# Hybrid decoder layer: the output projection and its norms join the FFN's listed order, token tiles are reordered, the third f pair's first products come earlier

## The chip, the cores and the metric

One core of one Trainium2 chip. The metric is the device time of one execution in microseconds (us), and the kernel is compared with the one before it on the same chip. TensorE (PE in the profile) multiplies, VectorE (DVE) and ScalarE (ACT) do the elementwise work, GpSimd (POOL) computes the small powers of the norms and issues accumulating DMAs, SyncE (SP) issues the other DMAs.

## The reference, cut to what matters

One layer on 1024 tokens of width 1024. The change sits between the mixing branch and the feed-forward part:

```python
merged = jax.nn.sigmoid(g_att) * y_att + jax.nn.sigmoid(g_conv) * y_conv
x = x + rms_norm(merged @ w_out[l], norm_mix_post[l])

h = rms_norm(x, norm_ffn_pre[l])
u = causal_dwconv(h @ w_up[l], conv_ffn_w[l])          # 1024 -> 2 x 2816
a, g = jnp.split(u, 2, axis=-1)
f = (jax.nn.gelu(g, approximate=True) * a) @ w_down[l]
x = x + rms_norm(f, norm_ffn_post[l])
```

## The kernel before

All products run in float16 with each operand split into a high and a low half; a product is three passes (`PASSES`): high by high, high by low, low by high. A split is one ScalarE instruction for the high half and one VectorE instruction for the low half (`split`, L98 and L99; `halves` in the FFN, L1383 and L1385). Large products are cut in two by two blocks and done with seven block products instead of eight, so sums and differences of blocks are made first.

The order of work comes about in two ways. Most of the kernel hands its instructions to the compiler's scheduler, which arranges each engine's instructions by their dependencies and by program order. Inside `tc.manual_schedule` the order of the named engines is as written. In the FFN a planner (`Plan`) writes it: every step is a job with an engine, a cost, the buffers that it reads and writes (`Buf`, each from a pool with so many tiles) and a due time; the products of TensorE have a fixed sequence (`seq=True`), and `order` places all other jobs around them by a simulation of the five engines, of the DMA and of the pools. `DUE` and `AHEAD` say how late or how early a job may be placed. TensorE's other jobs (transposes, the one-column sums `pr` over partitions) stand where that simulation finds them ready.

The passage that the change concerns, in the kernel before, is left to the compiler's scheduler:

- `wsplit("wo", ...)` splits the eight row tiles of w_out (`wh_wo`), and the last gate pair g7 finishes; `m16[k]` holds the two halves of the merged activations.
- `out_proj(tt)` for each token tile of 128: 48 matmuls into two PSUM banks `py` (L1180), ScalarE's square with a row sum (L1182), VectorE's eviction into `hn` (L1183), the first norm (a power on GpSimd, L183), the residual into `x` (L1187) and its store, the square for the second norm (L59), and the normed tile `hn` (L1190).
- `blocks(tt, h)`: eight transposes of `hn` into two banks `pt` (L1198). For tiles 0 to 3 the two halves of the blocks b11 and b21 are made (L1206, L1207); for tiles 4 to 7 the sums t1, t2, t3, t4 and b22 (L1212 to L1224), with slots `tb` and `hb`. Products 1 and 2 of a pair read tiles 0 to 3; products 3 to 7 need tiles 4 to 7 too (product 5 reads t1).
- An f pair is 128 columns of a and 128 of g of w_up. `pair_fetch`, `pair_sums` and `pair_split` load and split its weights: two staging tiles of the pool `ws` (4 tiles, shared with the x tiles `xr`), a slot `s12`, and four tiles of the pool `wh` (8 tiles). Of the first two pairs the products 1, 2 and 5 are issued here (L2089), after that the list takes over with products 6, 7, 3 and 4 (L1458). Products 1 and 2 use one bank (a), 6, 7 and 4 another (b), 5 and 3 a third (c); each product is evicted before the next one on its bank begins.

The pools that bind the passage: 16 slots `s` (eight hold w_out, four of the m16 tiles lie there), 4 tiles `x`, 4 `ws`, 8 `wh`, 8 PSUM banks.

## Time and profile before

| what | value |
|---|---|
| time, median of 3 runs | 1318.19 us (1316.74 to 1320.07) |
| the profiled execution's own time | 1317.39 us |
| its span | 1315.7 us |
| granted TensorE clock | 0.999 |
| TensorE busy | 1295.0 us |
| VectorE busy | 1096.7 us |
| ScalarE busy | 941.6 us |
| output projection's matmuls (L1180) | 602.4 to 690.3 us from the start |

Busy times are those of instructions; a matmul's end is modelled, so busy shares of TensorE are a little high, and its gaps a little larger than shown. The row of an instruction in the timeline reads: start, duration, engine, line, operation, output <- inputs, shapes, count, and in brackets the engine's idle time before it with what ended it.

### The profile page before, as it was taken

How to read it: one execution, taken by the hardware profiler on the slowest of the kernel's cores; microseconds unless marked ns; L12 is line 12 of the kernel's file. 1: busy time of each engine (PE TensorE's matmuls, PEld its weight loads, DVE VectorE, ACT ScalarE, POOL GpSimd, SP SyncE). 2: the span in 40 equal slices, each digit the busy share in tenths (PEclk: the TensorE clock that was granted, in tenths of full speed). 3: DMA queues.
4: the chain of work that ended last, by engine and by line, in shares of the span. 5: the costliest groups of instructions: out<-in, count | busy, mean ns of one | idle time of the engine just before them, and what ended most of it. 6: DMA issues, size and time to landing. Idle time of an engine off the chain costs nothing.

```text
span 1315.7 us, 16998 instructions
## 1 busy us (share of the span) xinstructions
PE 1295.0 (98%) x6406; PEld 581.5 (44%) x6406; DVE 1096.7 (83%) x1762; ACT 941.6 (72%) x1336; POOL 85.6 (7%) x120
## 2 busy tenths in 40 slices
PE   8999999999999999999999999999999999999997
PEld 4444444444444444444444444444444444444443
DVE  6578988888878967877799999789879879979986
ACT  7578878787778966675566767876977777787444
POOL 2000000000000000000110000100200210120103
PEclk9999999999999999999999999999999999999999
DMA  7111210111101223241330311611961692294807
GB/s 274 34 34 33 65 33 17 48 33 33 49 1 48 65 65 105 75 177 58 126 133 33 128 65 67 257 62 33 180 188 48 110 243 64 48 228 130 235 0 129
DMA packets 35541, 123.41 MB, mean 94 GB/s; under 512 B 4081, under 2 KB 4209, under 8 KB 35458
## 3 DMA queue, kind: packets, MB, share of 16 engines
q1 hardware_dynamic: 25088, 85.61, 19.3%
q0 software_dynamic: 10368, 36.70, 13.6%
q8 instruction: 50, 0.82, 0.3%
q14 instruction: 33, 0.27, 0.1%
q10 hardware_dynamic: 2, 0.00, 0.0%
HBM read 84.52 MB, written 37.78 MB: 93 GB/s over the span
## 4 chain that ended last, share of the span: by engine, by line
PE 54%; issue 24%; DVE 9%; DMA 6%; ACT 5%; POOL 3%; POOLq 0%; DVEq 0%; SPq 0%; ACTq 0%
PE py L1180 5%; PE pcb L212 3%; PE pcc L212 3%; PE pcx L212 3%; PE pq L212 3%; PE pk L212 3%; PE pywa L806 3%; PE pywc L806 3%; PE pd L1689 2%; PE pd L1722 2%; PE A L834 2%; POOL acc L1349 2%; PE o L834 2%; PE z L834 2%; DMA yacc<-acc 2%
## 5 line engine op out<-in xcount | busy, mean ns | idle before, releaser
L1458 PEld LDWEIGHTS <-wh_u 128*128 128x128 f16 x1776 | 172.0, 98 | 211.2 <-issue 3.3
L2089 PEld LDWEIGHTS <-wh_g 128*128 128x128 f16 x588 | 56.9, 98 | 69.4 <-issue 1.1
L1623 ACT ACTIVATE st<-pq,sd 128x512 f32<-128x512 f32 x112 | 72.3, 695 | 18.1 <-PE pq L1619 16.0
L1180 PE MATMUL py<-wh_wo,m 128*128 128x512 f16 x384 | 83.7, 379 | 0.0
L877 ACT ACTIVATE sh<-sp 128x1024 f16<-128x1024 f32 (+3 forms) x48 | 40.4, 842 | 52.2 <-DVE sp L872 52.0
L1385 DVE SCALAR_TENSOR_TENSOR wh_u<-ws_u,sc_u,wh_u 128x1024 f16<-128x1024 f32 (+1 forms) x60 | 65.5, 1102 | 7.8 <-ACT wh_u L1383 7.6
L1349 POOL DMA_DIRECT2D acc<-st x56 | 43.2, 772 | 431.1 <-ACT st L1623 430.8
L1383 ACT ACTIVATE wh_u<-ws_u,sc_u 128x1024 f16<-128x1024 f32 (+1 forms) x60 | 59.4, 1004 | 4.1 <-DVE sc_u L1368 3.9
L872 DVE TENSOR_TENSOR sp<-A,sp 1x1024 f32<-1x1024 f32 (+3 forms) x40 | 35.9, 897 | 29.9 <-PE A L834 26.5
L59 ACT ACTIVATE jk_u<-ws_u 128x1024 bf16<-128x1024 f32 x44 | 46.2, 1049 | 15.6 <-DMA ws_u<-w_up_nt 15.4
L881 DVE TENSOR_TENSOR sh<-sp,sh 128x1024 f16<-128x1024 f32 (+3 forms) x48 | 45.8, 955 | 13.5 <-ACT sh L877 13.3
L1180 PEld LDWEIGHTS <-m 128*128 128x128 f16 x384 | 37.4, 98 | 44.2
L1492 DVE SCALAR_TENSOR_TENSOR ua<-ca,cw_a,ua 128x1023 f32<-128x1023 f32 (+1 forms) x40 | 51.2, 1279 | 1.6 <-ACT ua L1490 1.5
L907 DVE SCALAR_TENSOR_TENSOR w<-e,w 128x1024 f16<-128x1024 f32 (+3 forms) x48 | 45.8, 954 | 6.8 <-ACT w L903 6.7
L1492 DVE SCALAR_TENSOR_TENSOR ug<-cg,cw_g,ug 128x1023 f32<-128x1023 f32 (+1 forms) x40 | 51.1, 1277 | 0.1
L903 ACT ACTIVATE w<-e 128x1024 f16<-128x1024 f32 (+3 forms) x48 | 40.5, 844 | 14.7 <-DVE e L898 13.7
L898 DVE TENSOR_TENSOR e<-e,g 128x1024 f32<-128x1024 f32 (+3 forms) x48 | 45.7, 953 | 2.5 <-ACT g L894 2.5
L867 ACT ACTIVATE sp<-e,one 128x1024 f32<-128x1024 f32 (+3 forms) x48 | 44.4, 925 | 4.0 <-DVE e L862 2.7
L853 ACT ACTIVATE e<-z,cz 128x1024 f32<-128x1024 f32 (+3 forms) x48 | 43.1, 898 | 3.6 <-PE z L834 3.6
L212 PE MATMUL pcb<-hT,wh_cb 128*128 128x512 f16 x192 | 45.1, 380 | 0.0
L212 PE MATMUL pcx<-hT,wh_cx 128*128 128x512 f16 x192 | 44.9, 379 | 0.0
L212 PE MATMUL pk<-hT,wh_k 128*128 128x512 f16 x192 | 44.6, 380 | 0.0
(760 smaller groups left out, 3047.6 us busy)
## 6 DMA issues: line engine op xcount, KB each, us to landing
acc<-st POOLq DMA_DIRECT2D x56, 512.0 KB, 6.2
ws_u<-w_up_nt SPq DMA_DIRECT2D x44, 512.0 KB
ds<-w_down SPq DMA_DIRECT2D x22, 512.0 KB
ws_g<-w_in_nt SPq DMA_DIRECT2D x14, 512.0 KB
x<-x SPq DMA_DIRECT2D x8, 512.0 KB
ws_wo<-w_out SPq DMA_DIRECT2D x8, 512.0 KB
xr<-x SPq DMA_DIRECT2D x8, 512.0 KB
yacc<-acc SPq DMA_DIRECT2D x16, 256.0 KB
```

The source lines that it names most:

```text
L59: self.nc.scalar.activation(self.junk(f"jk_{name}"), src, AF.Square, accum_out=acc)
L212: nc.tensor.matmul(ps, w[:, wi, ds(k * P, P)], hT[:, hi, k, ds(c * NH, NH)], start=n == 0, stop=n == last)
L806: nc.tensor.matmul(ps, w[0][:, wi, ds((d % 2) * NH + k * P, P)], acts[bi][k][:, hi, ds(c * NH, NH)], start=n == 0, stop=n == 11)
L834: nc.tensor.matmul(out, w, mv, skip_group_check=True, **kw)
L1180: nc.tensor.matmul(ps, m16[k][:, hi, ds(tt * P, P)], wo[k][:, wi, sl], start=k == 0 and p == 0, stop=k == 7 and p == 2)
L1349: j = pl.add(eng, 0.45 if eng == "SP" else 1.14, lambda: e.dma_start(dst(), srcf(), **kw), r, [b] if w is None else w, ahead=AHEAD["load"] ...
L1383: A(C["As" if big else "Ash"], lambda: act.activation(dst.t[:, 0, dsl], src.t[:, ssl], AF.Copy, scale=sb.t["s"]), [(src, sreg), sb], [(dst ...
L1385: V(C["V" if big else "Vh"], lambda: vec.scalar_tensor_tensor(dst.t[:, 1, dsl], src.t[:, ssl], sb.t["s"], dst.t[:, 0, dsl], ALU.mult, ALU. ...
L1458: pe.matmul(b.t, p.w[wt].t[:, wi, ds(wc * NH + k * P, P)], pr.block(i, h, k), start=first and n == 0, stop=n == 3 * KH - 1, skip_group_che ...
L1492: V(C["V"], lambda lag=lag: vec.scalar_tensor_tensor(u.t[:, lag:], c.t[:, :T - lag], sm.t[:, 2 - lag:3 - lag], u.t[:, lag:], ALU.mult, ALU ...
L1623: A(C["Ah"], lambda tt=tt, b=b, st=st: act.activation(st.t[:, tt % 2, :], b.t, AF.Copy, scale=q.sd.t[:, 0:1]), [b, q.sd], [(st, str(tt % 2 ...
L2089: nc.tensor.matmul(ps, w[wt][:, wi, ds(wc * NH + k * P, P)], self.block(i, hi, k), start=first and n == 0, stop=n == 3 * KH - 1, skip_grou ...
```

## The change

The output projection, its norms, the transposes and the token blocks become jobs of the planner and stand in the listed order together with the FFN; the old functions that left them to the compiler's scheduler go. The token tiles are taken in the order 0, 1, 2, 4, 3, 5, 6, 7; the first three run together, k by k. The weights of the first three f pairs are split in the list (`EARLY` lets their loads and splits be placed any time ahead). Products 1 and 2 of the third pair come ahead of the first pair's product 5, and the second pair's product 5 goes back to its place behind product 6. Three pools of small tiles get their sizes in the planner, and the planner starts with times at which the w_out tiles, the last m16 tile, ScalarE and VectorE become available. For tiles 4 to 7 the first differences read an SBUF copy of the transposed tile where they read PSUM before.

```diff
+PRE = ((0, 1), (1, 1), (0, 2), (1, 2), (2, 1), (2, 2), (0, 5))
+TORDER = (0, 1, 2, 4, 3, 5, 6, 7)
...
-        def out_proj(tt):
-            xt = xr.pop(tt)
-            sm = self.small(f"r_post{tt}")
...
-            for nh in range(2):
-                ps = self.bank(f"py{tt}_{nh}")
-                sl = ds(nh * NH, NH)
-                for k in range(8):
-                    for p, (hi, wi) in enumerate(PASSES):
-                        nc.tensor.matmul(ps, m16[k][:, hi, ds(tt * P, P)], wo[k][:, wi, sl],
-                                         start=k == 0 and p == 0, stop=k == 7 and p == 2)
-                nc.scalar.activation(jk[:, sl], ps, AF.Square, scale=sgn[:, 24:25], accum_out=sm[:, 3 + nh:4 + nh])
-                nc.vector.scalar_tensor_tensor(h[:, sl], ps, sgn[:, 24:25], gp[:, sl], ALU.mult, ALU.mult)
...
-            nc.sync.dma_start(self.x2[tt], y)
-            r2 = self.rstd_of(y, f"ffn{tt}")
-            nc.vector.scalar_tensor_tensor(h, y, r2, gf, ALU.mult, ALU.mult)
-            return h
...
-        def blocks(tt, h):
...
-            nc.vector.scalar_tensor_tensor(tb[0][:, 0], p3[0], s_h2, b11[:, 0], ALU.mult, ALU.subtract)
-            nc.vector.tensor_tensor(tb[0][:, 0], tb[0][:, 0], b11[:, 1], ALU.subtract)
-            halves(t1, tb[0][:, 0])
...
-        for tt in range(8):
-            if tt + 1 < 8:
-                load_xr(tt + 1)
-            hs[tt] = out_proj(tt)
-            if tt == 0:
-                self.pair_split("u0")
-                self.pair_fetch("u1")
-            if tt == 3:
-                self.pair_sums("u1")
-                self.pair_split("u1")
-            if tt == 5:
-                self.pair_fetch("u2")
-            for t in {2: (0,), 4: (1, 2), 5: (3, 4), 6: (5,), 7: (6,)}.get(tt, ()):
-                blocks(t, hs[t])
+        self.passage = m16, wo, xr, gp, gf, s_h2, sgn[:, 24:25]
         self.pairs = {f: Up(self, f) for f in range(NFF)}
-        p0, p1 = self.pairs[0], self.pairs[1]
-        p0.prod(1)
-        p0.prod(2)
-        p1.prod(1)
-        with tc.high_priority():
-            blocks(7, hs[7])
-        p1.prod(2)
-        p1.prod(5)
-        p0.prod(5)
 
...
+    FIRST, EARLY = 3, 200.0
...
-        pl = Plan(dict(s=16, ws=4, wh=8, o16=4, x=4, pm=8))
-        C = dict(A=0.97, Ah=0.5, As=1.04, Ash=0.6, Aq=1.18, V=1.21, Vh=0.64, Vp=0.72)
+        pl = Plan(dict(s=16, ws=4, wh=8, o16=4, x=4, pm=8, sm=8, rb=8, sc=16))
+        C = dict(Asq=0.82, A=0.97, Ah=0.5, As=1.04, Ash=0.6, Aq=1.18, V=1.21, Vh=0.64, Vp=0.72)
...
+
+        DUE = {"conv": 20.0, "fin": 25.0, "ev": 3.0, "pass": 5.0, "hn": 14.0}
...
+        m16 = [given("o16" if d < 4 else "s", t) for d, t in enumerate(m16t)]
+        wo = [given("s", t) for t in wot]
+        gp, gf = given("x", gpt), given("x", gft)
+        xr = {tt: given("ws", t) for tt, t in xrt.items()}
+        hn, prods = {}, {}
+        for k in range(8):
+            wo[k].avail = (0.0, 1.2, 4.2, 5.4, 8.0, 9.2, 10.4, 11.6)[k]
+        m16[7].avail = 13.0
+        pl.begin = {"A": 11.5, "V": 13.0}
...
+        def out_proj(tt):
...
+            for nh in range(2):
+                sl, reg, b = (lo, hi)[nh], "lh"[nh], ps[nh]
+
+                def mm(ks, b=b, sl=sl):
+                    for k in ks:
+                        for p, (h_, w_) in enumerate(PASSES):
+                            pe.matmul(b.t, m16[k].t[:, h_, ds(tt * P, P)], wo[k].t[:, w_, sl],
+                                      start=k == 0 and p == 0, stop=k == 7 and p == 2)
+                prods[tt, nh] = lambda ks, mm=mm, b=b: pl.add("PE", 0.65 * len(ks), lambda: mm(ks), [m16[k] for k in ks] +
+                                                              [wo[k] for k in ks], [b], seq=True)
+            yield
+            for nh in range(2):
+                sl, reg, b = (lo, hi)[nh], "lh"[nh], ps[nh]
+                A(C["Asq"], lambda b=b, sl=sl, nh=nh: act.activation(self.junk(f"jk_n_post{tt}")[:, sl], b.t, AF.Square,
+                                                                     scale=s_py, accum_out=sm.t[:, 3 + nh:4 + nh]),
+                  [b], [(sm, reg)], due=DUE["pass"])
+                V(C["Vp"], lambda b=b, sl=sl: vec.scalar_tensor_tensor(h.t[:, sl], b.t, s_py, gp.t[:, sl], ALU.mult, ALU.mult),
+                  [b, gp], [(h, reg)], due=DUE["pass"])
+
...
+            V(C["V"], lambda: vec.scalar_tensor_tensor(y.t, h.t, sm.t[:, 2:3], xr[tt].t, ALU.mult, ALU.add), [sm, h, xr[tt]], [y])
+            load("SP", None, lambda: self.x2[tt], lambda: y.t, r=[y], w=[], ahead=1e9)
...
+            pl.add("G", 0.6, power, [], [sm])
+            V(C["V"], lambda: vec.scalar_tensor_tensor(h.t, y.t, sm.t[:, 2:3], gf.t, ALU.mult, ALU.mult), [sm, y, gf], [h],
+              due=DUE["hn"])
...
+            def turn(e):
+                def f():
+                    for k in range(KH):
+                        pe.transpose(pt[e].t[:, ds(k * P, P)], h.t[:, ds((e * KH + k) * P, P)], self.ident)
+                return f
+            for e in range(2):
+                pl.add("PE", 0.45, turn(e), [h], [pt[e]])
...
+            for e in range(2):
+                A(C["Ah"], lambda e=e: act.activation(hbt.t[:, e], p3(e), AF.Copy, scale=s_h2), [pt[e]], [(hbt, str(e))])
+            t0, t1_ = part(tb[0], 0), part(tb[0], 1)
+            tt_(tb[0], 0, part(hbt, 0), lambda: ap["b11"][:, 0], ALU.subtract, [(hbt, "0"), (o_, "b11")])
+            tt_(tb[0], 0, t0, lambda: ap["b11"][:, 1], ALU.subtract, [(o_, "b11")])
+            two("t1", tb[0], 0)
...
         def up_weights(f):
+            ah, al, aq = (self.EARLY,) * 3 if f < 3 else (AHEAD["up"], None, AHEAD["sq"])
...
+            sq = Buf("sm", lambda: self.small(f"sm_{n}"))
+            summed = n in self.praw
+            if summed:
+                sm, ta, tg, ts = self.praw.pop(n)
+                sq = given("sm", sm)
...
-            s12 = slab(f"s12_{n}")
+            s12 = given("s", ts) if summed else slab(f"s12_{n}")
             w = p.w = [Buf("wh", lambda i=i: self.wh.tile([P, 2, D], F16, tag="wh", name=f"wh_{n}_{i}")) for i in range(4)]
...
+            if not summed:
+                comb(s12, lo, ug, lo, ug, hi, ALU.add, ahead=ah)
+                comb(s12, hi, s12, lo, ua, lo, ALU.subtract, ahead=ah)
+                comb(ug, lo, ua, lo, ug, lo, ALU.subtract, ahead=ah)
...
-            p, pr = up[f], prs[f]
-            if f < 2:
-                p.ca, p.cg, p.ug = given("s", pr.ca), given("s", pr.cg), given("s", pr.ug)
-                p.bank = {"c": given("pm", pr.ps["c"])}
-            else:
-                p.ca, p.cg, p.ug = slab(f"ca{f}"), slab(f"cg{f}"), slab(f"ug{f}")
-                p.bank = {b: Buf("pm", lambda b=b: self.bank(f"pu{f}{b}")) for b in "ac"}
-            p.bank["b"] = Buf("pm", lambda: self.bank(f"pu{f}b"))
+            p = up[f]
+            p.ca, p.cg, p.ug = slab(f"ca{f}"), slab(f"cg{f}"), slab(f"ug{f}")
+            p.bank = {b: Buf("pm", lambda b=b: self.bank(f"pu{f}{b}")) for b in "abc"}
...
-            pl.add("PE", 2.6, mm, [p.w[wt]], [b], seq=True)
+            pl.add("PE", 2.6, mm, [p.w[wt]] + [(hb[tt], BLOCK[i]) for tt in (range(4) if i < 3 else range(4, 8))], [b], seq=True)
...
-            for f in range(NFF):
-                up_weights(f) if f < 3 else None
-            for f in range(2):
+            for n, tt in enumerate(TORDER):
+                load_xr(tt)
+                if n == 0 or n >= self.FIRST:
+                    op = out_proj(tt)
+                    next(op)
+                if n >= self.FIRST:
+                    for nh in range(2):
+                        prods[tt, nh](range(8))
+                elif n == 0:
+                    rest = [out_proj(t) for t in TORDER[1:self.FIRST]]
+                    for r in rest:
+                        next(r)
+                    for k in range(8):
+                        for t in TORDER[:self.FIRST]:
+                            for nh in range(2):
+                                prods[t, nh]((k,))
+                for _ in rest.pop(0) if 0 < n < self.FIRST else op:
+                    pass
+                blocks(tt)
+                for f in {0: (0,), 2: (1,), 5: (2,)}.get(n, ()):
+                    up_weights(f)
+            for f in sorted({f for f, _ in PRE}):
                 up_open(f)
+            for f, i in PRE:
+                up_prod(f, i)
...
-                    if f >= 2:
+                    if (f, 1) not in PRE:
...
-                        if f >= 2 or i not in (5, 2):
+                        if (f, i) not in PRE:
...
-            j.t0 = 0.0
+            j.t0 = max([0.0] + [b.avail for b in j.bufs])
...
-        eng = {e: 0.0 for e in self.LAG}
+        eng = {e: self.begin.get(e, 0.0) for e in self.LAG}
```

More of the change, by code (lines that the diff above doesn't have):

```diff
@@ L1251, in mixer @@
[L1251 to L1260 removed]
+        xr = {tt: self.ws.tile([P, D], F32, tag="ws", name=f"xr{tt}") for tt in TORDER[:2]}
+        for tt in xr:
+            nc.sync.dma_start(xr[tt], a["x"][ds(tt * P, P), :])
+        self.passage = m16, wo, xr, gp, gf, s_h2, sgn[:, 24:25]
@@ L1354, in tot @@
         def tot(n, sm, cnt, slack, keep):
-            b, rb, ps, st = note(), note(), Buf("pm", lambda: self.bank(f"pr_{n}")), {}
+            b, rb, ps, st = Buf(None if keep else "sc", lambda: {}), Buf("rb", lambda: {}), Buf("pm", lambda: self.bank(f"pr_{n}")), {}
             def pre():
@@ L1397, in ffn @@
         fall = slice(0, T)
-        uw, up = {}, {}
+        up = {}
+        hb = [note() for _ in range(8)]
+        BLOCK = {1: "b11", 2: "b21", 3: "b22", 4: "t4", 5: "t1", 6: "t2", 7: "t3"}
+        m16t, wot, xrt, gpt, gft, s_h2, s_py = self.passage
+        m16 = [given("o16" if d < 4 else "s", t) for d, t in enumerate(m16t)]
[3 more added lines that the diff above has]
+        hn, prods = {}, {}
@@ L1710, in down_last @@
                 o = slab(f"o{tt}")
-                sm = Buf(None, lambda tt=tt: self.small(f"fin{tt}"))
+                sm = Buf("sm", lambda tt=tt: self.small(f"fin{tt}"))
                 y = yb_[tt]
@@ L1830, in __init__ @@
     def __init__(self, pool, make):
[L1831 removed]
+        self.pool, self.make, self.tile, self.log, self.left, self.avail = pool, make, None, [], 0, 0.0
     @property
@@ L1851, in __init__ @@
     def __init__(self, caps):
-        self.jobs, self.caps, self.now = [], caps, 0.0
+        self.jobs, self.caps, self.now, self.begin = [], caps, 0.0, {}
     def add(self, eng, cost, fn, r=(), w=(), seq=False, ahead=1e9, due=1e9):
```

124 lines of the change are left out of this document (62 added, 62 removed).

## The prediction

> **What bounds the kernel now.** I read the page first: how much of the span TensorE, the busiest engine, is without work.
>
> ```profile
> span 1315.7 us, 16998 instructions
> PE 1295.0 (98%) x6406; PEld 581.5 (44%) x6406; DVE 1096.7 (83%) x1762; ACT 941.6 (72%) x1336; POOL 85.6 (7%) x120
> ```
>
> TensorE is idle for 1315.7 - 1295.0 = 20.7 us. The change neither adds nor takes away a matmul, so it can win only a part of these 20.7 us, and lose whatever new waits it makes. The next view, busy time by stretch, says where they lie (columns: PE, PEld, DVE, ACT, POOL busy; clock; DMA).
>
> ```profile
> 0.00:20.00 20.00, 15.96 (x56) 8.07 (x57) 12.57 (x32) 15.64 (x24) 5.26 (x19) 1.00 0.88 350
> 20.00:560.00 540.00, 538.30 (x2859) 233.74 (x2858) 431.15 (x720) 408.19 (x567) 4.62 (x5) 1.00 0.16 49
> 560.00:602.00 42.00, 41.40 (x195) 18.68 (x194) 31.05 (x59) 27.07 (x42) 1.30 (x2) 1.00 0.43 154
> 602.00:634.00 32.00, 32.00 (x153) 14.78 (x152) 25.19 (x31) 20.38 (x29) 1.11 (x2) 1.00 0.21 66
> 634.00:690.00 56.00, 56.00 (x284) 28.12 (x283) 48.92 (x84) 33.75 (x65) 9.29 (x12) 1.00 0.39 132
> 690.00:712.00 22.00, 20.25 (x101) 9.78 (x100) 21.25 (x37) 14.79 (x26) 2.01 (x2) 1.00 0.14 48
> 712.00:730.00 18.00, 16.44 (x79) 7.44 (x78) 16.39 (x31) 8.78 (x10) 0.00 (x0) 1.00 0.10 30
> 730.00:1260.00 530.00, 526.30 (x2460) 238.27 (x2459) 469.56 (x699) 387.92 (x535) 48.94 (x63) 1.00 0.49 128
> 1260.00:1316.00 56.00, 48.32 (x234) 22.60 (x232) 40.59 (x75) 25.09 (x46) 13.05 (x15) 0.97 0.46 76
> ```
>
> The output projection (602 to 690) has no TensorE idle time at all: nothing can be won there, only lost. Idle are 1.75 us in 690 to 712 and 1.56 us in 712 to 730, together 3.31 us, and 3.70 us in the 530 us that the list orders already (0.7 us per 100 us). The first 602 us (4.04 + 1.70 + 0.60) lie before the change, and the 7.68 us of the last stretch are the closing chain of the last token tile, which it leaves alone. So 3.31 + 3.70 = 7.0 us are within reach, 0.5% of the time. The waits around the change, in the view of who waited for whom from 595 to 730:
>
> ```profile
> PE pt L1198 <- DVE hn L1190: 1.0, 1, 1.0
> PE pu0b L1458 <- DVE sc_u L1366: 0.8, 1, 0.8
> PE pu1b L1458 <- DVE cau L1464: 0.8, 1, 0.8
> PE pu0a L2089 <- ACT cgu L2104: 0.7, 1, 0.7
> ```
>
> **Head of the projection.** The timeline of TensorE and VectorE where it begins:
>
> ```profile
> 602.37 2.48 DVE L99 SCALAR_TENSOR_TENSOR wh_wo<-ws_wo,sc,wh_wo 128x1024 f16<-128x1024 f32 x2 [0.91 <-ACT wh_wo L98]
> 602.39 0.59 PE L1180 MATMUL py<-wh_wo,m 128*128 128x512 f16 x2
> ...
> 602.84 3.40 PE L1180 MATMUL py<-wh_wo,m 128*128 128x512 f16 x15
> ```
>
> The low half of the first w_out tile is ready only at about 602.37 + 1.28 = 603.65 (two in 2.48 us). TensorE doesn't notice: its order was chosen freely, and it runs what needs only the high half first. The new list writes the order down: for each k, for each of three tiles and two halves, the passes high-high, high-low, low-high. The second matmul needs the low half; it stood at about 602.6 and can start at 603.65. Loss: 1.05 us, once (bounds 0, if the halves come earlier, and 1.3, one whole low split). Later k don't wait: six banks times three passes are 18 x 0.216 = 3.9 us of matmuls per k (0.216 from the row below), against 1.28 us of VectorE per low half. Nor does the interleaving of three tiles win anything: the row of 15 shows matmuls running on while VectorE still makes w_out, so the old order already mixes tiles.
>
> The Trainium skill, page "TensorE: Matmul & The Clock Gate", section "Step-by-step: what each phase is for", says that matmuls stay in program order and that only weight loads are pulled ahead. By that rule the 1.05 us stand; were it wrong, the sum below would be 1.05 us lower.
>
> **Matmuls and transposes.** The counts stay:
>
> ```profile
> L1180 PE MATMUL py<-wh_wo,m 128*128 128x512 f16 x384 | 83.7, 379 | 0.0
> ...
> L1198 PE MATMUL pt<-ident,hn 128*128 128x128 f32 x64 | 8.1, 274 | 1.0 <-DVE hn L1190 1.0
> ```
>
> 384 in a row come to 83.7 us, 0.216 to 0.218 each, and 64 transposes to 8.1 us, about 1 us a tile: no difference. What changes is where the transposes stand. The list puts them where it believes the normed tile hn ready, between projection jobs of 24 matmuls (5.2 us); if hn is later than believed, TensorE stops. Tile 0's chain in the trace:
>
> ```profile
> 624.41 0.69 ACT L1182 ACTIVATE jk_n_post<-py,sgn 128x512 bf16<-128x512 f32 x1 [4.44 <-PE py L1180]
> ...
> 625.22 1.42 DVE L1183 SCALAR_TENSOR_TENSOR hn<-py,sgn,g_post 128x512 f32<-128x512 f32 x2 [2.96 <-ACT jk_n_post L1182]
> ...
> 631.02 1.28 DVE L1190 SCALAR_TENSOR_TENSOR hn<-x,r_ffn,g_ffn 128x1024 f32<-128x1024 f32 x1 [0.66 <-POOL r_ffn L183]
> ```
>
> From 624.41 to 632.30 it takes 7.9 us on free engines. The list's costs and lags for the same steps (two squares, statistics, power, residual, square, statistics, power, gain) add up to 8.8 us, so it errs on the safe side by 0.9 us, and rounding up to the next 5.2 us boundary adds on average half of that. One thing it does not know: the second row shows VectorE starting on the bank only after ScalarE's 0.69 us on it, though both only read. The Trainium skill, "PSUM — Partial Sum Buffer", section "Terms", counts two reads of one bank at once as a collision, which is the wait this row shows. That is 0.7 us inside the 0.9 us of margin. I price the risk at the rate of the stretch that is listed already, 0.7 us per 100 us over about 110 us: 0.8 us (bounds 0, and 8 us if each tile's transposes wait the 1.0 us of the first row of waits).
>
> **Norms, blocks, weights.** The same instructions as before, except that tiles 4 to 7 take the first difference from an SBUF copy: nothing on TensorE. VectorE was busy 48.92 of 56 us and 21.25 of 22 us, so I check it at the spot where TensorE first needs the last tile's t1. The timeline there: TensorE's products, the VectorE row that ends that t1 (704.59), and rows that the next part needs:
>
> ```profile
> 691.52 2.75 PE L2089 MATMUL pu0a<-hA,wh_u 128*128 128x512 f16 x12
> 694.11 2.75 PE L2089 MATMUL pu1a<-hA,wh_u 128*128 128x512 f16 x12
> 697.60 2.75 PE L2089 MATMUL pu0a<-hA,wh_u 128*128 128x512 f16 x12 [0.74 <-ACT cgu L2104]
> 701.37 1.06 PE L1198 MATMUL pt<-ident,hn 128*128 128x128 f32 x8 [1.01 <-DVE hn L1190]
> ...
> 704.59 0.68 DVE L1213 TENSOR_TENSOR hB<-tb,hB 128x512 f16<-128x512 f32 x1
> 704.86 0.38 PE L2089 MATMUL pu1c<-hB,wh_u 128*128 128x512 f16 x1
> ...
> 713.47 0.15 DVE L1366 TENSOR_SCALAR sc_u<-pr_u 128x1 int32<-128x1 int32 x1
> 713.61 2.76 PE L1458 MATMUL pu0b<-hB,wh_u 128*128 128x512 f16 x12 [0.78 <-DVE sc_u L1366]
> 713.83 1.15 ACT L1383 ACTIVATE wh_u<-ws_u,sc_u 128x1024 f16<-128x1024 f32 x1 [1.93 <-DVE sc_u L1368]
> ...
> 717.01 1.28 DVE L1385 SCALAR_TENSOR_TENSOR wh_u<-ws_u,sc_u,wh_u 128x1024 f16<-128x1024 f32 x1
> ...
> 724.95 2.75 PE L1458 MATMUL pu1b<-hB,wh_u 128*128 128x512 f16 x12 [0.78 <-DVE cau L1464]
> ```
>
> t1 is done at 705.27. In the new kernel VectorE starts the evictions of tiles 0 to 2 about 6 us later (all three tiles finish with the last k, which begins at 603.4 + 7 x 3.9 = 630.7) and has by 634 some 1.5 us less behind it (of tile 0's chain it has done 1.42 + 2 x 1.28 and 0.3 of small ones there, 4.3 us; in the new order about four evictions of 0.71, 2.8 us); the third pair's first weight split moves ahead of this point (1.28 us, and five instructions of 0.15 for its scale, 0.7 us): t1 at about 708.8. TensorE asks for it two products later than now (2 x 2.59 us, the distance 691.52 to 694.11), plus 1.05 for the head, plus 1.15 of waits named below, less 0.74 and 1.01: at about 704.86 + 5.6 = 710.5. It is in time by 1.7 us. SyncE's queue runs in the listed order as well, and a load that waits for one of the four staging buffers holds back the x2 stores behind it; the stores free the buffers of later tiles, and that is part of the 0.8 us.
>
> **The products moved.** Price of each step, from the rows above. Removed: the 1.01 us wait for the last tile's hn (two more products, 5.2 us, cover it); the 0.74 us at the second pu0a (a product lies between, and the list sees ScalarE's queue); the 0.78 us before pu1b, since the second pair's product 5 now stands between its 6 and 7. Kept: the 0.78 us before pu0b, where 6 and 7 still follow each other on one bank. Added: products 1 and 2 of the third pair, adjacent on one bank, 0.8 us by those rows (bounds 0, if transposes fall between them, and 1.3); and a wait for the third pair's first weights. The eight weight buffers are full with two pairs, so this split starts when the first pair's product 2 is done, and has one product to hide behind. By the rows of 713.83 and 717.01 it takes 2.43 us plus hand-overs, against 2.59 us; an instruction already running on either engine adds up to 1.3 us each. I take 0.35 (bounds 0 and 2.6).
>
> **The sum.** +1.05 - 1.01 - 0.74 - 0.78 + 0.80 + 0.35 + 0.80 = +0.47 us. Behind 730 the list is made anew, with the same work; I leave its 3.70 us as they are (bounds: half gone or half as much again, 1.85 either way). The profiled execution took 1317.39 us (span 1315.7 and 1.7 around it), within the runs' 1316.74 to 1320.07, whose median is 1318.19. So 1317.39 + 0.47 = 1317.9 for such an execution, and **1318.6 us** against the median. With all small terms at their kind ends (head kept, no new waits, half of the rest gone) the case reaches down to 1315, with a doubled list risk and more waits behind 730 up to 1322.
>
> **Rivals.** *VectorE becomes the bound at the end of the passage (slower).* The point is the margin of 1.7 us at t1. The second pair's split runs today when VectorE has room:
>
> ```profile
> 649.17 1.28 DVE L99 SCALAR_TENSOR_TENSOR wh_u<-ws_u,sc,wh_u 128x1024 f16<-128x1024 f32 x1
> 650.37 0.69 DVE L1292 TENSOR_TENSOR s_u<-s_u,ws_u 128x512 f32<-128x512 f32 x1
> ...
> 656.36 0.74 DVE L99 SCALAR_TENSOR_TENSOR wh_u<-ws_u,sc,wh_u 128x512 f16<-128x512 f32 x1
> ```
>
> It is three full low halves, a half one and four differences: 3 x 1.28 + 0.74 + 4 x 0.69 = 7.3 us. In the list its loads share the four staging buffers with x tiles that are due earlier; if the split slides behind the last tiles' norms, t1 comes 7.3 us later, and TensorE waits 7.3 - 1.7 = 5.6 us: 1318.6 + 5.6 = 1324.2. For it speaks VectorE's 97% in 690 to 712, against it its 7 idle us in 634 to 690.
>
> *The list clears nearly all of it (faster).* No wait from the list in the passage, and the new order clears the 3.70 us behind 730 too: +1.05 - 2.53 + 0.80 - 3.70 = -4.4 us, 1313.8. For it: waits there are single ones of 0.9 to 1.0 us that hang on neighbours in a queue. Against it: stretches that the list orders today keep their 0.7 us per 100.
>
> ```profile
> PE pq L1619 <- ACT st L1623: 1.8, 5, 0.9
> PE pu21b L1458 <- DVE cg L1464: 1.0, 1, 1.0
> PE pu5b L1458 <- DVE ca L1464: 0.9, 1, 0.9
> ```
>
> **How the numbers follow.** A measurement of this kernel tells about 0.3% (4 us) from no change: the three runs lie 3.3 us apart. The forecast has 0.5, nearly all of it within 4 us of 1318.2; the faster rival 0.25, the slower one 0.25, both mostly beyond. Eight in ten run from 1312.5 (the faster rival and a little of its bounds: no head wait) to 1325.5 (the slower one and 1.3 for the weights). The likeliest case's own range is 1315 to 1322.
>
> **What would show it.** In the profile after: the second py matmul about 1 us behind the first; TensorE idle near 3.8 us from 602 to 730, with no wait on hn above 1 us; pu2a at about 705 instead of 730; 0.8 us before the second pu2a and before pu0b's second use, none before pu1b's. I am wrong if transposes wait one after another on hn (the list believed too much), if pu0c waits for VectorE (the slower rival), or if the stretch from 730 to 1260 keeps less than 2 us or more than 6 us.

## The result and the profile after

The changed kernel takes 1311.34 us (median of 6 runs, 1310.01 to 1313.53) against 1318.96 us (1316.74 to 1320.53) of the kernel before on the same chip: ratio 0.9944, 95% interval 0.9931 to 0.9957. It is 7.6 us faster. The prediction said 1318.6 us and 1312.5 to 1325.5, so the result lies below its range.

The profiled execution took 1310.93 us, against 1317.39 us before. Its page, the lines that answer to those shown of before:

```profile
span 1309.1 us, 17012 instructions
PE 1293.0 (99%) x6406; PEld 580.1 (44%) x6406; DVE 1097.0 (84%) x1762; ACT 940.7 (72%) x1336; POOL 86.7 (7%) x120
...
PE 93%; DVE 3%; ACT 2%; DMA 1%; issue 1%; SPq 0%; POOL 0%; POOLq 0%; DVEq 0%; ACTq 0%
```

The last row is the chain that ended last. It now runs through TensorE for 93% of the span. The same row of the kernel before:

```profile
PE 54%; issue 24%; DVE 9%; DMA 6%; ACT 5%; POOL 3%; POOLq 0%; DVEq 0%; SPq 0%; ACTq 0%
```

Busy time by stretch after, in the stretches of the prediction:

```profile
560.00:602.00 42.00, 42.00 (x199) 19.00 (x197) 30.84 (x55) 26.90 (x42) 1.30 (x2) 1.00 0.41 150
602.00:634.00 32.00, 31.59 (x148) 14.26 (x147) 22.73 (x27) 15.34 (x19) 0.00 (x0) 1.00 0.12 34
634.00:690.00 56.00, 56.00 (x287) 28.39 (x285) 50.77 (x92) 38.44 (x74) 10.90 (x14) 1.00 0.49 150
690.00:712.00 22.00, 20.82 (x106) 10.31 (x105) 21.43 (x36) 16.54 (x31) 2.32 (x2) 1.00 0.17 50
712.00:730.00 18.00, 17.22 (x81) 7.73 (x80) 16.84 (x28) 10.81 (x14) 0.00 (x0) 1.00 0.20 59
730.00:1260.00 530.00, 530.00 (x2483) 240.11 (x2481) 475.74 (x712) 387.61 (x532) 48.99 (x63) 1.00 0.48 127
```

TensorE's idle time fell from 3.31 to 1.18 + 0.78 = 1.96 us in 690 to 730, rose from 0 to 0.41 us at the head of the projection, and went from 3.70 us to nothing in the 530 us behind 730, which the list ordered before the change too. The passage that was rewritten gives about 1 us; most of the gain appears where no product was moved.

The records hide a little of each wait, since a matmul's end is modelled. In the two pu2a rows below, 3.93 us lie between the starts; twelve matmuls take 2.59 us, so the wait cost 1.34 us where 1.18 us is shown. Counted in this way from the starts of all matmuls (0.216 us each when nothing waits), the 6.6 us of span come to 4.9 us behind 730, 1.2 us in 602 to 730 and 0.5 us ahead of 602. The last is 0.8 us less at a wait of gate pair 7 and 0.3 us more at the start of the kernel. That wait was between nothing and 1.4 us in the profiles of the other kernels here, whose work up to there is the same, so I put it down to chance.

TensorE's timeline at the places that the prediction named, with VectorE's row that ends the last tile's t1:

```profile
601.99 0.38 PE L1348 MATMUL py<-wh_wo,m 128*128 128x512 f16 x1
602.78 1.46 PE L1348 MATMUL py<-wh_wo,m 128*128 128x512 f16 x6 [0.41 <-DVE wh_wo L101]
...
702.93 2.75 PE L1482 MATMUL pu2a<-hA,wh_u 128*128 128x512 f16 x12
706.86 2.75 PE L1482 MATMUL pu2a<-hA,wh_u 128*128 128x512 f16 x12 [1.18 <-ACT cg L1491]
707.38 1.89 DVE L1414 TENSOR_TENSOR hB<-tb,hB 128x512 f16<-128x512 f32 x3
709.45 2.75 PE L1482 MATMUL pu0c<-hB,wh_u 128*128 128x512 f16 x12
...
715.57 2.75 PE L1482 MATMUL pu0b<-hB,wh_u 128*128 128x512 f16 x12 [0.78 <-DVE ca L1488]
```

The waits on hn, at the second pu0a and before pu1b are gone. The two products of pu2a follow each other on one bank and wait, as do those of pu0b. The first pu0c, product 5, starts without a wait: t1 is the second of the three halves from 707.38 and so ready at about 708.6.

### The profile page after: what moved, and what is told of

The parts are those of the page before. It is cut to its first block, busy times and chain, and to the rows that moved or that the text cites. A ratio compares the mean times of both kernels' runs of the same rounds, so it can differ in the third digit from the quotient of the medians.

```text
span 1309.1 us, 17012 instructions
## 1 busy us (share of the span) xinstructions
PE 1293.0 (99%) x6406; PEld 580.1 (44%) x6406; DVE 1097.0 (84%) x1762; ACT 940.7 (72%) x1336; POOL 86.7 (7%) x120
## 3 DMA queue, kind: packets, MB, share of 16 engines
q0 software_dynamic: 10368, 36.70, 13.7%
## 4 chain that ended last, share of the span: by engine, by line
PE 93%; DVE 3%; ACT 2%; DMA 1%; issue 1%; SPq 0%; POOL 0%; POOLq 0%; DVEq 0%; ACTq 0%
PE pq L1641 11%; PE py L1348 6%; PE pcb L214 3%; PE pcc L214 3%; PE pcx L214 3%; PE pq L214 3%; PE pk L214 3%; PE pywa L808 3%; PE pywc L808 3%; PE A L836 2%; PE pd L1711 2%; PE o L836 2%; PE pd L1744 2%; PE z L836 2%; PE pv L409 1%; PE pv L447 1%
## 5 line engine op out<-in xcount | busy, mean ns | idle before, releaser
L1482 PEld LDWEIGHTS <-wh_u 128*128 128x128 f16 x1848 | 178.8, 98 | 217.9 <-issue 2.5
L1305 DVE SCALAR_TENSOR_TENSOR wh_u<-ws_u,sc_u,wh_u 128x1024 f16<-128x1024 f32 (+1 forms) x66 | 72.4, 1103 | 12.4 <-ACT wh_u L1303 12.0
L1303 ACT ACTIVATE wh_u<-ws_u,sc_u 128x1024 f16<-128x1024 f32 (+1 forms) x66 | 66.4, 1006 | 22.6 <-DVE sc_u L1288 10.2
L1514 DVE SCALAR_TENSOR_TENSOR ua<-ca,cw_a,ua 128x1023 f32<-128x1023 f32 (+1 forms) x44 | 56.2, 1277 | 1.2 <-ACT ua L1512 1.1
L1514 DVE SCALAR_TENSOR_TENSOR ug<-cg,cw_g,ug 128x1023 f32<-128x1023 f32 (+1 forms) x44 | 56.1, 1276 | 0.8 <-ACT ug L1512 0.7
```

What stands on the lines that cost most here:

```text
L1303: A(C["As" if big else "Ash"], lambda: act.activation(dst.t[:, 0, dsl], src.t[:, ssl], AF.Copy, scale=sb.t["s"]), [(src, sreg), sb], [(dst ...
L1305: V(C["V" if big else "Vh"], lambda: vec.scalar_tensor_tensor(dst.t[:, 1, dsl], src.t[:, ssl], sb.t["s"], dst.t[:, 0, dsl], ALU.mult, ALU. ...
L1482: pe.matmul(b.t, p.w[wt].t[:, wi, ds(wc * NH + k * P, P)], pr.block(i, h, k), start=first and n == 0, stop=n == 3 * KH - 1, skip_group_che ...
L1514: V(C["V"], lambda lag=lag: vec.scalar_tensor_tensor(u.t[:, lag:], c.t[:, :T - lag], sm.t[:, 2 - lag:3 - lag], u.t[:, lag:], ALU.mult, ALU ...
```

## What the waits behind 730 were

A wait on TensorE there begins elsewhere. VectorE and ScalarE work through a written order, so an instruction that waits for a transfer holds back everything behind it. VectorE's waits for the second staging tile of a pair, in the kernel before:

```profile
957.51 0.69 DVE L1390 TENSOR_TENSOR s_u<-ws_u 128x512 f32<-128x512 f32 x1 [2.58 <-DMA ws_u<-w_up_nt]
1069.12 0.69 DVE L1390 TENSOR_TENSOR s_u<-ws_u 128x512 f32<-128x512 f32 x1 [5.75 <-DMA ws_u<-w_up_nt]
1179.26 0.69 DVE L1390 TENSOR_TENSOR s_u<-ws_u 128x512 f32<-128x512 f32 x1 [6.60 <-DMA ws_u<-w_up_nt]
```

and in the changed one:

```profile
952.66 0.69 DVE L1310 TENSOR_TENSOR s_u<-ws_u 128x512 f32<-128x512 f32 x1 [3.46 <-DMA ws_u<-w_up_nt]
1060.05 0.69 DVE L1310 TENSOR_TENSOR s_u<-ws_u 128x512 f32<-128x512 f32 x1 [3.52 <-DMA ws_u<-w_up_nt]
1068.37 0.69 DVE L1310 TENSOR_TENSOR s_u<-ws_u 128x512 f32<-128x512 f32 x1 [1.74 <-DMA ws_u<-w_up_nt]
```

Near 955 and between 1060 and 1069 us they come in both; near 1179 VectorE waits in the kernel before alone. At these places the down products add their partial sums to memory, and the DMA engines are almost fully taken (busy share 0.97 and 0.98 in 920 to 960 and 1030 to 1070 of the kernel before). The page "PSUM — Partial Sum Buffer" of the Trainium skill, section "Engine vs sequencer instructions", calls the queues of ScalarE and VectorE strictly first in, first out; the rows agree, in the idle time before each of them VectorE starts nothing else. ScalarE, too, waited in the kernel before, and a bank of the down products behind it:

```profile
928.05 1.15 ACT L1383 ACTIVATE fx<-ua,sp_f 128x1024 f16<-128x1024 f32 x1 [0.46 <-DMA acc<-st]
932.00 1.15 ACT L1383 ACTIVATE fx<-ua,sp_f 128x1024 f16<-128x1024 f32 x1 [0.61 <-DMA acc<-st]
936.58 0.69 ACT L1623 ACTIVATE st<-pq,sd 128x512 f32<-128x512 f32 x1 [1.25 <-PE pq L1619]
942.65 1.46 PE L1619 MATMUL pq<-wq,fy 128*128 128x512 f16 x6 [0.95 <-ACT st L1623]
```

From 936.58 ScalarE works without a gap until TensorE gets its bank. The profile puts the 1.25 us before that row down to TensorE, but a store issued at 927.89 landed at 936.50, and in the kernel with plain stores below the same instruction (there at 932.65) has no wait; so it most likely waited for that landing.

The clearest case is in the profile of the second experiment below (natural tile order), where the stall is long enough to be followed through:

```profile
1077.08 0.69 DVE L1310 TENSOR_TENSOR s_u<-ws_u 128x512 f32<-128x512 f32 x1 [7.84 <-DMA ws_u<-w_up_nt]
1081.59 0.16 DVE L1282 CAST rb_u<-sc_u 128x1 bf16<-128x1 f32 x1
...
1081.80 0.17 PE L1291 MATMUL pr_u<-rb_u,ones 128*128 128x1 bf16 x1 [3.16 <-DVE rb_u L1282]
1081.82 4.44 PE L1482 MATMUL pu14b<-hA,wh_u 128*128 128x512 f16 x12
```

VectorE stands 7.84 us, gets to rb_u late, and TensorE stands 3.16 us at the one-column sum and pu14b behind it.

## The experiments

The theories. *Late landings:* the waits behind 730 come from transfers that land late in front of VectorE and ScalarE, and the new order lets fewer of them through. *The right start* ('right picture' in the expectations): the list works better now because it knows when the passage begins. *The product sequence* ('products', later theory A): it is the third pair's products, moved forward, that do it. *A draw* ('redraw', later theory B): any other order of the same list may do as well, and the kernel before had a poor one.

**The old product sequence in the new list.**

```diff
-PRE = ((0, 1), (1, 1), (0, 2), (1, 2), (2, 1), (2, 2), (0, 5))
+PRE = ((0, 1), (0, 2), (1, 1), (1, 2), (1, 5), (0, 5))
```

> The changed kernel with the products ahead of the list's main part as they were: (0,1), (0,2), (1,1), (1,2), (1,5), (0,5); the rest of the change stays. Theory 'right picture' (the gain behind 730 us comes from the passage standing in the list, so that the list knows where each engine is): TensorE's idle time behind 730 us stays under 1 us (3.70 before, 0 after), and only 690 to 730 gets worse, 1.96 to some 4 us: 1313 to 1314 us. Theory 'redraw' (any change of the list's input draws its waits anew, between 0 and 5 us): behind 730 us anything from 0 to 5, time 1311 to 1318. Theory 'products' (moving the third pair's products is what takes the waits away): behind 730 us back to 3 to 4 us, time 1315 to 1317.

1318.15 us, ratio 1.0003 (0.9992 to 1.0014): the whole gain is gone. Who waited for whom on TensorE:

```profile
PE pu14b L1482 <- DVE cg L1488: 2.3, 1, 2.3
PE pu1c L1482 <- ACT hB L1413: 1.4, 1, 1.4
PE pu1b L1482 <- DVE ca L1488: 1.2, 1, 1.2
PE pu0b L1482 <- DVE sc_u L1281: 1.1, 1, 1.1
```

Idle are 4.76 us in 690 to 730 and 2.96 us behind. In this order, listing the projection wins nothing by itself.

**Token tiles in natural order.**

```diff
-TORDER = (0, 1, 2, 4, 3, 5, 6, 7)
+TORDER = (0, 1, 2, 3, 4, 5, 6, 7)
```

> The changed kernel with the token tiles in the order 0 to 7. 'Right picture': idle behind 730 us under 1 us, 602 to 730 within 1 us of the changed kernel's 2.4, time 1311 to 1312. 'Redraw': 0 to 5 us behind 730, time 1311 to 1317. 'Products': as the changed kernel.

1313.99 us, 0.9972 (0.9959 to 0.9985): slower than the changed kernel, and the intervals don't overlap. The passage is nearly as good (2.30 us idle in 690 to 730). The profiled execution was the longest of its ten, 1317.93 us; behind 730 it has 3.22 us idle, nearly all of it the 3.16 us wait shown above. 'Products' expected the changed kernel's time and missed; only 'redraw' had room for this.

**No start times.** The changed kernel without the times at which the w_out tiles, the last m16 tile and two engines become available.

```diff
-            wo[k].avail = (0.0, 1.2, 4.2, 5.4, 8.0, 9.2, 10.4, 11.6)[k]
+            wo[k].avail = 0.0
-        m16[7].avail = 13.0
-        pl.begin = {"A": 11.5, "V": 13.0}
```

> The changed kernel without the times at which the w_out tiles, the last m16 tile, ScalarE and VectorE become available: the list believes all of them free at its start. 'Right picture': the list is up to 13 us wrong at the start, waits come back in the passage (1 to 4 us in 602 to 690, TensorE for the sums of the first pair or for transposes), and behind 730 us nothing or little, since by then list and chip have met. 'Redraw': 0 to 5 us behind 730.

1310.87 us, 0.9948 (0.9934 to 0.9963), no idle time behind 730, and 0.93 us in 602 to 690 where the changed kernel has 0.41. The gain does not need the start times. This run alone does not refute the theory of the right start, which allowed for it; the first experiment speaks against it: there the list had the start times, and 2.96 us stayed.

**The second pair's product 5 alone.** The kernel before with this product back behind product 6; the rest of the change isn't made.

```diff
         p1.prod(2)
-        p1.prod(5)
         p0.prod(5)
...
-                        if f >= 2 or i not in (5, 2):
+                        if f >= 2 or i not in (5, 2) or (f, i) == (1, 5):
```

> The kernel before with one part of the change alone: the second pair's product 5 goes back behind its product 6, all else as before. All theories: the 0.78 us before the second pair's product 7 goes, so 712 to 730 drops from 1.56 to about 0.8 us of idle time. Behind 730 us: 'right picture' 3 to 4.5 us as before, time 1317 to 1318.5; 'redraw' 0 to 5 us, time 1314 to 1319; 'products' 3 to 4.

1318.02 us, 1.0005 (0.9991 to 1.0018). The wait before pu1b goes, but the cover in front of pu0b goes with it (2.07 us there). Behind 730 the profile, of the longest of the runs (1323.24 us), has 5.66 us.

**The third pair's products not moved forward.**

```diff
-PRE = ((0, 1), (1, 1), (0, 2), (1, 2), (2, 1), (2, 2), (0, 5))
+PRE = ((0, 1), (1, 1), (0, 2), (1, 2), (0, 5))
```

> The changed kernel without the third pair's products 1 and 2 ahead of the rest (the second pair's product 5 stays in its new place). TensorE then reaches the first pair's product 5 two products (5.2 us) earlier, before VectorE has the last tile's t1. My margin put it 1.7 us late for TensorE's need with them, so 1.7 - 5.2 = 3.5 us of waiting without; the 1.2 us between the two pu2a go. 690 to 730: idle 1.96 + 3.5 - 1.2 = about 4.3 us. If that is all ('cover'), time 1311.3 + 2.3 = 1313.6 and nothing behind 730. 'Late landings': some 0 to 4 us behind 730 besides, as it falls.

1319.55 us, 0.9999 (0.9986 to 1.0012): the whole gain is gone, and the 1313.6 us of 'cover' were a miss. In front of pu0c TensorE now waits for the last t1:

```profile
704.45 1.04 PE L1387 MATMUL pt<-ident,hn 128*128 128x128 f32 x8
709.04 0.49 PE L1482 MATMUL pu0c<-hB,wh_u 128*128 128x512 f16 x1 [3.56 <-ACT hB L1413]
710.01 2.29 PE L1482 MATMUL pu0c<-hB,wh_u 128*128 128x512 f16 x5 [0.49 <-DVE hB L1414]
```

The two products of 2.59 us are the cover for the last tile's blocks, and without them 4.05 us show. The idle time in 690 to 730 is 4.82 us, near the 4.3 expected; but the granted clock fell behind the wait (last section), so that the passage lost 4.4 us against the changed kernel counted by starts, and 1.59 us stand behind 730.

**Plain stores in the kernel before.** The down products' partial sums are written instead of added to memory; the sums over the groups are left out. The order of every engine stays as it was.

```diff
-                    kw = {} if g == 0 else dict(accum_op=ALU.add)
+                    kw = {}
```

> The kernel before with its accumulating stores of the quarter products made plain stores: the sums over the groups are left out, the order of instructions on every engine is the same. The stores move fewer bytes, so weight loads beside them can land earlier. Theory 'late landings' (TensorE's waits behind 730 us come from VectorE and ScalarE, whose queues run in order, standing before a load or store that lands later than the list believes): VectorE's wait for ws_u behind 730 falls from 16.5 to under 10 us, TensorE's waits before pq (1.8 us) and pu21b (1.0) go, the one before pu5b (0.9, which the list itself has) stays; time about 1314 to 1315 us. Theory 'order' (the waits lie in the listed order itself): 3.7 us of idle time stay, time 1317 to 1318.5.

1314.46 us, 0.9967 (0.9957 to 0.9976). A store took 6.2 us from issue to landing in the kernel before (first line, median of 56), and half of that here (second line):

```profile
acc<-st POOLq DMA_DIRECT2D x56, 512.0 KB, 6.2
...
acc<-st POOLq DMA_DIRECT2D x56, 512.0 KB, 3.0
```

VectorE's waits for ws_u fall from 16.5 to 3.6 us, the waits at pq go, and 1.60 us of 3.70 are left behind 730: pu5b, as expected, and pu21b, which was expected to go.

**Plain stores in the changed kernel**, the same edit.

> The changed kernel with the stores of the down products' partial sums written plainly instead of added to memory (it leaves out the sums over the groups of w_down rows); every engine keeps its order. Theory 'late landings': the changed kernel has no idle time on TensorE behind 730 us that those landings could cause, so nothing is left to win: 1310 to 1312 us, ratio to the kernel before 0.994, idle in 730 to 1260 still 0. Rival 'lighter stores speed up everything' (the 4 us of the same edit in the kernel before have another cause, at the end of the kernel or in the memory as a whole): the changed kernel gains the same 4 us, about 1307, ratio 0.991.

1311.02 us, 0.9949 (0.993 to 0.9969): no different from the changed kernel. Plain stores helped only where TensorE had waits to lose.

**The old product sequence with plain stores**, both edits in the changed kernel.

> The changed kernel with the old sequence of the first pairs' products (its profile had 4.8 us idle in 690 to 730 and 3.0 us behind 730) and plain stores (sums over the groups left out). Theory 'late landings': the 3 us behind 730 go and the 4.8 us in the passage stay: about 1315.2 us, ratio 0.997. Rival 'the order of the instructions alone makes the waits behind 730': they stay, about 1318, ratio 1.000.

1314.65 us, 0.9972 (0.9961 to 0.9982), as the theory of late landings said. The two stretches behind 690, here

```profile
690.00:730.00 40.00, 35.35 (x171) 16.71 (x170) 39.00 (x68) 25.10 (x40) 2.33 (x2) 1.00 0.18 53
730.00:1260.00 530.00, 530.00 (x2482) 240.53 (x2481) 473.08 (x703) 389.56 (x532) 35.59 (x63) 1.00 0.36 127
```

show the passage's 4.65 us untouched and nothing behind it. With the landings taken away, the old sequence costs 1314.65 - 1311.02 = 3.6 us, nearly all of it in the passage (4.65 us idle there against 1.93, 3.3 us of difference counted by starts).

**Other draws.** The list's costs for ScalarE changed by 2 or 3 per cent give another order of the same work.

```diff
-        AHEAD.update(self.ahead_set)
+        AHEAD.update(self.ahead_set, ca=1.02)
```

Of the changed kernel, with 1.02, 0.98 and 1.03:

> The changed kernel with ScalarE's costs 2% higher in the list: another order of the vector engines' work from the same rules, TensorE's sequence of products the same. 'Redraw' (any change of the list's input draws the waits behind 730 anew): 0 to 5 us there, time 1311 to 1316. If the gain is owed to the change's own order: under 1 us there and 1310.5 to 1312.

> The changed kernel with the list's ScalarE costs times 0.98: another order of everything from 602 us on, the product sequence kept. Theory A, the product sequence clears the waits behind 730 in any draw: idle in 730 to 1260 at most 0.3 us, time 1310 to 1313. Theory B, each draw is a draw (the kernel before and its redraws had 3.70, 0.22, 2.99 in their profiles): idle 0 to 4 us, more likely above 1 us than not, time 1311 to 1316.

> The changed kernel with the list's ScalarE costs times 1.03, the product sequence kept. Theory A: idle in 730 to 1260 at most 0.3 us, time 1310 to 1313. Theory B: idle 0 to 4 us, time 1311 to 1316.

Of the kernel before, with 1.02, 0.98 and 1.03:

> The kernel before with ScalarE's costs 2% higher in the list, nothing else. 'Redraw': 0 to 5 us of idle time behind 730 us, time 1313 to 1319; if the gain is owed to the change's own order, 3 to 4.5 us as before and 1317 to 1319.

> The kernel before with the costs of ScalarE in the list times 0.98, so that its listed order behind 730 is drawn anew; the passage up to 730 is left to the scheduler as before. Theory 'it depends on the draw how much of the late landings reaches TensorE': something between 1314.5 (no idle time behind 730) and 1320 (as much as half more than before), idle in 730 to 1260 and time moving together. Rival 'the listed passage is what clears the waits behind 730': idle there stays 3 us or more, time 1317 or above.

> The kernel before with the list's ScalarE costs times 1.03. Theory A: idle behind 730 around 2 to 4 us, time 1316 to 1319, as in most of its draws. Theory B: anything from 0 to 4 us, time 1314.5 to 1319.

Of the changed kernel with the old product sequence, with 0.98:

> The changed kernel with the old product sequence and the list's ScalarE costs times 0.98. The passage keeps its 4.8 us of idle time (690 to 730). Theory A, the product sequence decides: idle behind 730 stays near the 2.96 us of the first such kernel, time about 1318. Theory B, a draw: anything from 0 to 4 us, time 1314.5 to 1319.

Each ratio is to the kernel before as measured beside that kernel (medians of 1317.71 to 1319.01 us).

| kernel | time, us (range) | ratio to before (interval) | idle behind 730 in its profile, us |
|---|---|---|---|
| changed | 1311.34 (1310.01 to 1313.53) | 0.9944 (0.9931 to 0.9957) | 0 |
| changed, 1.02 | 1312.83 (1311.33 to 1313.86) | 0.9951 (0.9936 to 0.9967) | 0 (the longest run) |
| changed, 0.98 | 1311.01 (1310.08 to 1311.13) | 0.9948 (0.9933 to 0.9962) | 0 |
| changed, 1.03 | 1312.03 (1309.42 to 1314.03) | 0.9957 (0.9944 to 0.997) | 0 |
| before | 1318.96 (1316.74 to 1320.53) | 1 | 3.70 |
| before, 1.02 | 1315.25 (1312.2 to 1317.57) | 0.9975 (0.9962 to 0.9987) | 0.22 (the shortest run) |
| before, 0.98 | 1316.26 (1315.46 to 1318.89) | 0.9987 (0.9977 to 0.9996) | 2.99 (the shortest run) |
| before, 1.03 | 1315.08 (1312.46 to 1318.85) | 0.9979 (0.9967 to 0.999) | 0.31 (the shortest run) |
| old sequence in the list | 1318.15 (1316.37 to 1321.21) | 1.0003 (0.9992 to 1.0014) | 2.96 |
| old sequence, 0.98 | 1315.33 (1313.96 to 1319.29) | 0.9979 (0.9969 to 0.9989) | 0.74 |

Both theories have a part. A draw alone moves a kernel with the old sequence by 2 to 3 us, and the kernel before was the slowest of its four. But with the new sequence four draws out of four have no idle time there, and lie within 2 us of each other. The mean of the four ratios is 0.9950 for the new sequence and 0.9985 for the old one (1, 0.9975, 0.9987, 0.9979). Of the 0.56% gained, some 0.35%, or 4.6 us, goes with the new sequence and about 0.2%, or 2 to 3 us, with the draws, that is with luck; that it is the sequence and not the listing of the passage, the two kernels with the old sequence in the list say, whose mean is 0.9991. All kernels here with adding stores fit this: the seven with the third pair's products early (these four, natural tile order, no start times, and the last experiment) have ratios of 0.9934 to 0.9972, the eight without them 0.9975 to 1.0005, though the intervals of the nearest ones overlap. But the kernel with natural tile order, at 0.9972 and with 3.22 us behind 730, shows that the sequence does not clear the waits in every order and every execution. The expectation that the old sequence keeps 2 to 4 us in nearly every draw was a miss.

**High halves first, product 5 back.** The changed kernel; for the first k the passes that need only the high half of w_out run for all six banks first, and the first pair's product 5 returns behind its product 6.

```diff
-PRE = ((0, 1), (1, 1), (0, 2), (1, 2), (2, 1), (2, 2), (0, 5))
+PRE = ((0, 1), (1, 1), (0, 2), (1, 2), (2, 1), (2, 2))
...
+                        for ps_ in ((0, 2), (1,)) if k == 0 else ((0, 1, 2),):
-                                prods[t, nh]((k,))
+                                    prods[t, nh]((k,), ps_=ps_)
```

> The changed kernel with two further edits: for the first k of the projection the passes that need only the high half of w_out come first for all six banks, and product 5 of the first pair goes back to its place behind product 6. Theory: the 0.4 us wait at the second matmul of the projection goes, the wait before the first pair's product 6 (0.8 us) shrinks to 0.2; behind 730 the order is drawn anew, 0 to 3 us. 1310 us if the draw is kind, ratio 0.993; up to 1313 if not. Rival 'product 5 was needed as cover for the tokens of tiles 4 to 7': TensorE waits for them 2 us or more near 710, about 1313 with 0 behind 730.

1309.39 us (1308.2 to 1310.73), 0.9934 (0.9916 to 0.9953). Its stretches from 602:

```profile
602.00:690.00 88.00, 88.00 (x435) 42.96 (x434) 73.89 (x117) 55.27 (x94) 10.92 (x14) 1.00 0.34 106
690.00:730.00 40.00, 39.00 (x191) 18.70 (x190) 38.70 (x63) 28.34 (x44) 2.33 (x2) 1.00 0.18 57
730.00:1260.00 530.00, 529.75 (x2481) 240.25 (x2479) 474.92 (x713) 386.94 (x531) 49.09 (x63) 1.00 0.48 127
```

The wait at the head is gone and the pu0b wait too; only pu2a's 1.0 us is left in the passage. Its median is the lowest of all these kernels, though its interval overlaps that of the changed kernel.

## Why the prediction was wrong, point by point

**The step that failed** is the term for the stretch behind 730, the sentence "Behind 730 the list is made anew, with the same work; I leave its 3.70 us as they are (bounds: half gone or half as much again, 1.85 either way)". They went altogether, 4.9 us counted by starts, and less than 2 us there was one of the prediction's own signs of being wrong. Of the 7.1 us between the forecast +0.47 and the 6.6 us by which the span fell, 4.9 lie here, 1.7 in the passage and 0.5 ahead of 602. Two errors lie in the step. I took one profile's 0.7 us per 100 us as the rate of listed stretches; it was one draw, and other orders of the same list left as little as 0.22 and 0.31 us in 530 (in their shortest runs), and plain stores took 2.1 of the 3.70 us away; so more than half of it was no rate of the list but late landings that got through. And I treated the sequence up to 730 as ending at 730, while six of the seven kernels with the third pair's products early have at most 0.25 us in the 530 us behind it.

**The passage** was right in kind, and 1.4 us better in sum. By its terms:

| term | predicted, us | shown, us |
|---|---|---|
| head, second py matmul | +1.05 | +0.41 (0.9 in seven other listed kernels, 0.1 to 0.7 in three) |
| hn of the last tile, second pu0a, pu1b | -2.53 | -2.53, all three gone |
| the third pair's two products on one bank | +0.80 | +1.18 |
| the third pair's first weights | +0.35 | 0 (0.3 to 0.6 in three others) |
| list risk at the transposes | +0.80 | 0 (0.3 and 0.4 in two others) |
| sum | +0.47 | -0.94 |

At the head the second matmul stood behind the low half while others could have run, and putting the high passes first removed the wait. This agrees with the rule of program order that the page "TensorE: Matmul & The Clock Gate" of the Trainium skill gives in its section "Step-by-step: what each phase is for". The size of the wait depends on how far VectorE is when TensorE arrives. The 0.78 us before pu0b stayed, as said.

**The slower rival** didn't happen, but its place was the right one. t1 was ready at about 708.6, where 708.8 was predicted; TensorE asked at 709.45 instead of 710.5, so the margin was 0.8 us and not 1.7. Taking the two products away uncovered 4.05 us.

**The faster rival** is what happened, with 1313.8 us against 1311.34. Its sum was -4.4 us, the span fell by 6.6: counted by starts, it lacked 1.2 us behind 730, 0.5 us in the passage (the kinder head above all) and the 0.5 us ahead of 602. The argument against it, that listed stretches keep their rate, is the failed step again; I gave it 0.25 where the same profile held the reason for more: the waits at pq hung on a ScalarE queue that stood before transfers.

**Still open** is why the new sequence gives this slack. In the old sequence, too, loads are issued earlier once the passage is listed (near 949 and 1058 us by some 5 us), so that isn't enough. Nor are VectorE's waits gone: behind 730 it stands 16.5 us before ws_u in the kernel before, but also 15.7 us in the kernel without start times and 18.2 us in the last experiment, where TensorE has 0 and 0.25 us idle. So the transfers still land late, and what differs is how much of it reaches TensorE. The natural tile order, with the new sequence, had one execution with 3.2 us; whether that is the tile order or its draw is not tested. One profile for each kernel can't tell whether a particular lead of VectorE or ScalarE does it.

## What to carry to other kernels

A wait on the busiest engine in a listed stretch may be one draw of an order in front of transfers whose landings vary: redraw the order a few times before you call its idle time a rate, and before you credit a change with it. Price a moved product by a run with it and one without, not only by the wait beside it: here the third pair's two products were priced at 2.3 us and made 0.55%, some 7 us, of difference, in one order each. And where a written order replaces a free one, look for a first step in which work that needs only half of an operand can go first.

## What was not expected of the hardware

A wait of TensorE above about 2 us cost more than its length, because the granted clock fell behind it. The stretches around the 2.27 us wait at 1081.16 in the kernel with the old product sequence (PE busy, PEld, DVE, ACT, POOL; clock):

```profile
1076.00:1081.00 5.00, 2.89 (x14) 1.20 (x13) 2.37 (x3) 3.33 (x6) 0.00 (x0) 1.00 0.70 270
1081.00:1084.00 3.00, 2.83 (x10) 1.14 (x10) 2.73 (x7) 0.92 (x3) 0.00 (x0) 0.70 0.00 0
1084.00:1088.00 4.00, 4.00 (x17) 1.65 (x16) 3.62 (x4) 3.52 (x6) 0.00 (x0) 0.79 0.05 5
1088.00:1092.00 4.00, 4.00 (x20) 1.82 (x19) 3.93 (x12) 2.32 (x3) 0.00 (x0) 1.00 0.80 237
```

The mean clock is 0.70 and 0.79 in these 3 and 4 us; the fall itself is 3.41 us at 0.50 (1082.23 to 1085.64), and the product's twelve matmuls took 4.27 us instead of 2.75. It was the same behind the waits of 2.07, 2.09, 3.16 and 3.56 us (the twelve matmuls of pu14b above took 4.44 us), an extra 1.3 to 1.7 us each time. Behind waits of 1.41 to 1.59 us the clock stayed. In the kernel without the third pair's early products, whose profile has the 3.56 us, all ten runs have a mean clock of 0.996 or 0.997, where the changed kernel's six have 0.998 or 0.999. The page "TensorE: Matmul & The Clock Gate" of the Trainium skill, section "What's actually happening", puts the fall behind an idle window of about 3.4 us; here 2.07 us were enough, so the measurement decides. This makes the long waits dearer than the idle columns above show, and it was not in the prediction's prices.

A store that adds to memory took 6.2 us to land and a plain one 3.0 us. The expectation's "fewer bytes" is not what the profile counts: 36.70 MB on the stores' queue with both, but packets that took 13.6% of the DMA engines' time with adding and 8.6% with plain stores. That the loads beside them landed earlier with plain stores is seen only in the engines' shorter waits.
